# Expert products in halves of 512 columns, the scatter matrix by one comparison, and 22 large buffers

## The chip, the cores and the metric

The kernel runs on one core of one Trainium2 chip. The metric is the device time of one execution in microseconds (us). Before the change three runs took 841.2, 843.68 and 844.19 us; the median is 843.68. The engines are named as in the profile: PE is TensorE (matmuls; its weight loads are listed as PEld), DVE is VectorE, ACT is ScalarE, POOL is GpSimd, SP is SyncE, which issues the DMA transfers here.

## The reference

One decoder block on x of 512 tokens by 1024 channels, all float32: a first RMS norm, one input projection, a pooling mixer and a differential attention, two gates, an output projection with residual. Then the part that the change touches, a hierarchical mixture of 32 experts, of which each token uses two of one group:

```python
hn = rmsnorm(x, norm2_g)                      # 512 x 1024
pg = softmax(hn @ w_rg + b_rg)                # 4 groups, the best one is taken
pe = softmax((hn @ w_re + b_re)[its group])   # 8 experts, the best two
wts = p_top * pv / sum(pv)
hdn = silu(xb @ w_gate[e]) * (xb @ w_up[e])   # xb: the rows of hn that go to e; 1024 -> 512
y = (hdn @ w_down[e]) * wb                    # 512 -> 1024
out = x + (y added at its token's row)
```

## The kernel before

**Stages.** The first stage computes norm, projection, attention, pooling and output projection with float32r products in three passes (high and low parts of both operands). Its weights are loaded by `stage_to` (L141) and split into high and low parts by ACT and DVE in `split_to` (L154 and L155). Then come the router and the experts.

**The expert loop.** It begins at L1026 and takes the experts in 16 pairs, 0 to 15. Each expert has 64 slots (CAP); what goes beyond them is done in `run_overflow`, a loop that stands behind pair 6 (P_OVER) and takes as many turns as there are full blocks left, none with these inputs. The two experts of a pair share every PSUM bank: one has the upper 64 partitions, the other the lower 64.

Four experts form a group. `prep_P` builds the one-hot matrix P (token by slot) of a group with DVE, and `gather` (L851) multiplies hn with it on PE, which gives xT, the group's tokens by channel; this is done in the odd pairs for the next group. For a pair, in PE's order:

- gate and up (`ffn_in`, L881): 16 float32 matmuls each of 64 weight columns by 512 moving columns. The profile counts two records for each float32 matmul, so 32.
- `scatter_mats`: four matmuls with the identity (tile tp, L861) transpose P into PT, slot by token, copied by DVE (L863); four small matmuls (tile ws, L867) collect the slots' routing weights, which DVE adds into wv (L873).
- the gather of the next group, in odd pairs.
- `ffn_hT`: h = silu(gate) * up comes from ACT (L885) and DVE (L887); PE transposes it (ht, L894), DVE copies it to hT (L896).
- the last quarter of the pair before, scattered.
- `quarter_down` (L907), four quarters of 256 output columns: y on PE, its high part by ACT (L910), the low part by DVE (L911).
- `quarter_scatter` (L921), one quarter behind: PT times the high and the low part for four token blocks, in two banks; DVE adds each bank to the accumulator acc (L923).

**What sets the order.** The program is written out in its final order, and each engine works through its own list in order; semaphores come from the tile framework. Buffers are pools of equal tiles: 23 large ones of 8 KB a partition (tag S), 6 small ones of 2 KB (tag T) and 8 PSUM banks. A tile takes a buffer that is free in program order, and its first writer waits until the last reader of the old tile is done. In the expert loop acc, hn and xT hold five large buffers and the weight tiles the rest, 18. `prefetch(4)` stands behind gate, behind up and at the pair's end and issues four loads each time on SP's queue (L618); the first eighteen are issued in `out_proj` by the counts in PF. A pair uses twelve tiles: four each for gate, up and down. The last pair's down weights come as eight half tiles, one for each expert and quarter.

Of the kernel before, what the change touches and what calls it, by code (L numbers as in the profile page):

```python
# [27 lines left out]
CAP = 64  # L28
# [7 lines left out]
NBIG = 23  # L36
NSM = 6
# [4 lines left out]
PF = (6, 4, 3, 5)  # L42
# [5 lines left out]
def hybrid_block_kernel(  # L48
# [65 lines left out]
    # ---------------------------------------------------------------- loads  # L114
# [58 lines left out]
    # ---------------------------------------------------------------- constants  # L173
# [66 lines left out]
    # ---------------------------------------------------------------- first norm and transposes  # L240
# [24 lines left out]
    # ---------------------------------------------------------------- products in three float32r passes  # L265
# [20 lines left out]
    # ---------------------------------------------------------------- q, k, v  # L286
# [25 lines left out]
    # ---------------------------------------------------------------- attention  # L312
# [104 lines left out]
    # ---------------------------------------------------------------- pooling  # L417
# [28 lines left out]
    # ---------------------------------------------------------------- phase 1 program  # L446
# [146 lines left out]
    # ---------------------------------------------------------------- expert weights  # L593
# [27 lines left out]
    # ---------------------------------------------------------------- output projection, second norm, router  # L621
# [13 lines left out]
    Wst = const.tile([128, NT, NE, 2], F16, name="Wst")  # L635
# [199 lines left out]
    # ---------------------------------------------------------------- experts  # L835
# [5 lines left out]
    def gather(P, n, t0, t1, st, ks=(0, 1)):  # L841
        per = 512 // n
        if t0 == 0 and 0 in ks:
            st["b"] = [bank("xg", (128, per, n)) for _ in range(ND // per)]
            st["x"] = S([128, ND, n], name="xT") if ND * n > 512 else \
                T("xT")[:, :ND * n].rearrange("p (j s) -> p j s", j=ND)
        for k in ks:
            for i, b in enumerate(st["b"]):
                for t in range(t0, t1):
                    for j in range(per):  # L850
                        mm(b[:, j, :], hn[k][:, t, i * per + j, :], P(t),  # L851
                           start=t + k + j == 0, stop=t == NT - 1 and k == 1 and j == per - 1)
                if t1 == NT and k == 1:
                    jj = slice(i * per, (i + 1) * per)
                    tt(st["x"][:, jj, :], b, g2p[:, jj, None].to_broadcast([128, per, n]), op=OP.mult)
        return st["x"]

    def scatter_mats(Pp, np_, w):
        b = bank("tp", (128, 4, 128))
        for t in range(NT):  # L860
# [3 lines left out]
        bw = bank("ws")  # L864
        ne = w.shape[2]
        for t in range(NT):
            mm(bw[:np_, :2 * ne], Pp(t), w[:, t].rearrange("p e k -> p (e k)"), start=t == 0, stop=t == NT - 1)  # L867
        ws = small([128, 4], "ws")
        nc.vector.tensor_copy(ws[:np_, :2 * ne], bw[:np_, :2 * ne])
        wv = small([128, 1], "wv")  # L870
        for par in range(ne):
            s = slice(par * CAP, (par + 1) * CAP)
            ts(wv[s], ws[s, 2 * par:2 * par + 1], ws[s, 2 * par + 1:2 * par + 2], 1.0 / W_SCALE, op0=OP.add, op1=OP.mult)  # L873
        return PT, wv
# [16 lines left out]
    def ffn_hT(h, np_):  # L891
# [4 lines left out]
        nc.vector.tensor_copy(hTt[:, :, :np_], b[:, :, :np_])  # L896
# [29 lines left out]

    def take(w, e, part):
# [16 lines left out]
    # ---- blocks beyond the first CAP slots of an expert  # L944
# [33 lines left out]
    def run_overflow():  # L978
# [13 lines left out]
        with tc.For_i(0, n_over, 1) as i:  # L992
            e = nc.values_load(ov_i[0:1, ds(i, 1)], min_val=0, max_val=NE - 1)
            ts(rcol, R1[:, :, ds(e, 1)].rearrange("p t o -> p (t o)"), offs[:, ds(i, 1)], None, op0=OP.subtract)
            nc.vector.tensor_copy(wcol, Wst[:, :, ds(e, 1), :].rearrange("p t o k -> p t (o k)"))
# [29 lines left out]

    for p in range(NE // 2):  # L1026
# [3 lines left out]
        c0 = (p % 2) * 2 * CAP  # L1030
        xs = [st["x"][:, :, c0 + par * CAP:c0 + (par + 1) * CAP] for par in range(2)]
        bg_ = bank("gate")
# [3 lines left out]
        following = {}  # L1036
        if p % 2 == 1 and g + 1 < NE // 4:
            prep_P(g + 1, 0, NT, following)
# [12 lines left out]
        last_pair = p == NE // 2 - 1  # L1051
        halves = None if last_pair else [take("d", e, half) for half in range(2)]
        yq = {}
        for q in range(4):
            w = take("q", e, q) if last_pair else halves
            yq[q] = quarter_down(hTt, wv, w, q, 128)
            if q > 0:
                quarter_scatter(PT, q - 1, yq[q - 1], 128, last_pair)
        prev = (PT, 3, yq[3], 128, last_pair)
# [5 lines left out]
    quarter_scatter(*prev)  # L1065
# [25 lines left out]
```

## Time and profile before

| | |
|---|---|
| median of three runs | 843.68 us |
| span of the profiled execution | 844.5 us |
| that execution's own time | not given beside its span |
| PE busy | 813.4 us |
| DVE busy | 385.3 us |
| ACT busy | 202.5 us |
| moved by DMA | 234.15 MB |
| mean granted clock | 0.989 |

The span is the time from the first to the last instruction on the core. Busy time of an engine counts overlapping instructions once. Matmuls are pipelined: one lasts longer than the distance between two starts, so a mean duration is not what a matmul costs in a stream. The chain that ended last is followed back from the last instruction: at each step to what released it, or to the instruction before it on its engine. "Idle before" names the time in which the engine had nothing to do before an instruction, and what ended it. The granted clock is a share of TensorE's full 2.4 GHz.

### The profile page before, as it was taken

Reading aid. Unit: us, or ns where it says so; the run is one execution under the profiler, and the core shown is the slowest. Engines: PE = TensorE matmul, PEld = TensorE weight load, DVE = VectorE, ACT = ScalarE, POOL = GpSimd, SP = SyncE. Lnnn points to the kernel's source line nnn. Section 1 sums busy time; section 2 is a strip of 40 time slices with the busy share of each in tenths; the row PEclk is TensorE's granted clock in tenths of the full one; section 3 lists DMA queues with packets and bytes.
Section 4 is the critical chain, followed back from the end, with each engine's and each line's share of the span. In section 5 each row is a group of like instructions: output and inputs, shape, how many; then the busy total and the mean of one; then the engine's idle time right before and its main releaser. Section 6 shows DMA issues by size and latency. Waiting matters only on the chain. (4 is left out here: it accounts for less than half of the span.)

```text
span 844.5 us, 11816 instructions
## 1 busy us (share of the span) xinstructions
PE 813.4 (96%) x4822; PEld 531.8 (63%) x4822; DVE 385.3 (46%) x851; ACT 202.5 (24%) x405; POOL 36.4 (4%) x48
## 2 busy tenths in 40 slices
PE   7999999999999998999999999979999999999997
PEld 6887767778888877456456456446456456457444
DVE  5644495553555535743554244333253244335225
ACT  5544455445433424200010010000000010010010
POOL 1220050000000000000000000000000000000000
PEclk9999999999999999999999999989999999999999
DMA  9611103213266818589899999979999999999922
GB/s 317 208 51 50 50 11 111 79 50 100 88 226 252 331 50 331 210 328 426 352 426 426 379 425 424 385 285 427 386 427 425 382 426 426 381 427 425 410 74 100
DMA packets 54008, 234.15 MB, mean 277 GB/s; under 512 B 9920, under 2 KB 16576, under 8 KB 29888
## 3 DMA queue, kind: packets, MB, share of 16 engines
q1 hardware_dynamic: 53952, 233.37, 68.9%
q8 instruction: 39, 0.64, 0.3%
q14 instruction: 17, 0.14, 0.0%
HBM read 231.26 MB, written 2.10 MB: 276 GB/s over the span
## 5 line engine op out<-in xcount | busy, mean ns | idle before, releaser
L907 PE MATMUL y<-e,hT 128*64 128x256 f32 x1024 | 122.8, 388 | 3.2 <-DVE hT L896 3.2
L881 PE MATMUL gate<-e,xT 128*64 128x512 f32 x512 | 115.2, 603 | 4.9 <-DVE P L838 4.9
L881 PE MATMUL up<-e,xT 128*64 128x512 f32 x512 | 112.6, 592 | 0.0
L910 ACT ACTIVATE yq<-y,wv 128x256 fp32r<-128x256 f32 x64 | 30.4, 475 | 318.0 <-PE y L907 318.0
L887 DVE TENSOR_TENSOR h<-up,sg 128x512 f32<-128x512 f32 x16 | 17.0, 1062 | 183.2 <-PE up L881 113.5
L907 PEld LDWEIGHTS y<-e,hT 128*64 128x64 f32 x1024 | 70.1, 138 | 41.6 <-DVE hT L896 6.4
L881 PEld LDWEIGHTS up<-e,xT 128*64 128x64 f32 x512 | 36.7, 137 | 73.2 <-issue 73.2
L923 DVE TENSOR_TENSOR acc<-sc,acc 128x512 f32<-128x512 f32 x128 | 81.8, 681 | 0.2
L881 PEld LDWEIGHTS gate<-e,xT 128*64 128x64 f32 x512 | 35.8, 139 | 72.5 <-issue 69.7
L921 PE MATMUL sc<-yq,PT 128*128 128x256 f32 x512 | 77.4, 294 | 0.0
L921 PEld LDWEIGHTS sc<-yq,PT 128*128 128x128 f32 x512 | 64.8, 189 | 18.5 <-issue 18.5
L911 DVE SCALAR_TENSOR_TENSOR yq<-y,wv,yq 128x256 fp32r<-128x256 f32 x64 | 30.9, 484 | 86.9 <-ACT yq L910 86.9
L155 DVE SCALAR_TENSOR_TENSOR wl<-w,g1c,wh 128x512 fp32r<-128x512 f32 x64 | 48.9, 792 | 39.0 <-ACT wh L154 38.9
L282 PE MATMUL g<-hTh,wh 128*128 128x512 f32 x160 | 64.8, 405 | 0.1
L284 PE MATMUL g<-hTh,wl 128*128 128x512 f32 x160 | 62.4, 390 | 0.0
L283 PE MATMUL g<-hTl,wh 128*128 128x512 f32 x160 | 62.4, 390 | 0.0
L851 PE MATMUL xg<-P,hn 128*128 128x256 f16 x512 | 58.0, 272 | 0.5 <-DVE hn L672 0.4
L851 PEld LDWEIGHTS <-hn 128*128 128x128 f16 x512 | 49.2, 98 | 8.7 <-issue 2.1
L154 ACT ACTIVATE wh<-w,g1c 128x512 fp32r<-128x512 f32 x64 | 44.5, 719 | 1.0 <-DMA w<-in_w_in_dram 1.0
L885 ACT ACTIVATE sg<-gate 128x512 f32<-128x512 f32 x16 | 9.6, 597 | 122.3 <-PE gate L881 122.3
L282 PEld LDWEIGHTS g<-hTh,wh 128*128 128x128 f32 x160 | 30.0, 188 | 13.1 <-issue 5.4
L284 PEld LDWEIGHTS g<-hTh,wl 128*128 128x128 f32 x160 | 30.0, 188 | 6.5
(212 smaller groups left out, 983.6 us busy)
## 6 DMA issues: line engine op xcount, KB each, us to landing
e<-in_w_expert_gate_dram SPq DMA_DIRECT2D x64, 1024.0 KB, 10.1
e<-in_w_expert_up_dram SPq DMA_DIRECT2D x64, 1024.0 KB, 11.5
e<-in_w_expert_down_dram SPq DMA_DIRECT2D x60, 1024.0 KB, 13.7
w<-in_w_in_dram SPq DMA_DIRECT2D x16, 1024.0 KB, 5.4
w<-in_w_out_dram SPq DMA_DIRECT2D x4, 1024.0 KB, 5.8
e<-in_w_expert_down_dram SPq DMA_DIRECT2D x8, 512.0 KB, 9.0
x<-in_x_dram SPq DMA_DIRECT2D x4, 512.0 KB, 6.3
w<-in_w_pool_up_dram SPq DMA_DIRECT2D x2, 1024.0 KB, 4.8
```

The lines of the kernel that those rows point to most:

```text
L154: nc.scalar.mul(hi, src, g)
L155: stt(lo, src, g, f(hi), op0=OP.mult, op1=OP.subtract)
L282: mm(b, whi[:, k, s], ahi[:, k, :], start=first and k == 0, stop=False)
L283: mm(b, whi[:, k, s], alo[:, k, :], start=False, stop=False)
L284: mm(b, wlo[:, k, s], ahi[:, k, :], start=False, stop=last and k == 3)
L851: mm(b[:, j, :], hn[k][:, t, i * per + j, :], P(t), start=t + k + j == 0, stop=t == NT - 1 and k == 1 and j == per - 1)
L881: mm(b[s, :], xs[par][:, j, :], w[par][:, k, :], start=j == 0, stop=j == 7)
L907: mm(y[s, :], hTt[:, j, s], r, start=j == 0, stop=j == 3)
L910: nc.scalar.mul(yhl[:np_, 0], y[:np_], wv[:np_])
L911: stt(yhl[:np_, 1], y[:np_], wv[:np_], f(yhl[:np_, 0]), op0=OP.mult, op1=OP.subtract)
L921: mm(b[:, i, :], PT[:np_, t * 128:(t + 1) * 128], yhl[:np_, k, :], start=k == 0, stop=k == 1)
L923: tt(a, b, a, op=OP.add)
```

## The change

Pairs 0 to 14 compute the down product in two halves of 512 columns (`half_down`) instead of four quarters of 256. Each half is scattered by token blocks (`scatter_mms`), one bank for each block of 128 tokens, the high and the low part on the same weights. The first half is scattered behind both halves of y; the second is kept for the next pair, where three of its blocks stand behind up and the fourth behind ht. The four additions stand behind hT in the program. Pair 15 keeps its quarters.

PT is no longer transposed on PE. The weights tile Wst gets a third column, the token's number from 1 (`tok_id`, built by POOL); the ws matmuls (now `slot_info`, six columns) bring it to the slots along with the weights, and `scatter_mat` compares a row of all token numbers (`tok_row`) with it, in one DVE operation of 128 by 512. slot_info is called for both pairs of a group at once: in pair 0 for the first group, then in odd pairs behind the gather. hT is copied by ACT instead of DVE. P of the next group is built before gate instead of behind it. There are 22 large buffers instead of 23 and 8 small ones instead of 6; the last count of PF is 4 instead of 5, so 17 weight tiles are under way.

```diff
-NBIG = 23
-NSM = 6
+NBIG = 22
+NSM = 8
-PF = (6, 4, 3, 5)
+PF = (6, 4, 3, 4)
...
-    Wst = const.tile([128, NT, NE, 2], F16, name="Wst")
+    Wst = const.tile([128, NT, NE, 3], F16, name="Wst")
+    tok_id = const.tile([128, NT], F32, name="tok_id")
+    nc.gpsimd.iota(tok_id, pattern=[[128, NT]], base=1, channel_multiplier=1, allow_small_or_imprecise_dtypes=True)
+    nc.gpsimd.tensor_copy(Wst[:, :, :, 2], tok_id[:, :, None].to_broadcast([128, NT, NE]))
+    tok_row = const.tile([128, SEQ], F32, name="tok_row")
+    nc.gpsimd.iota(tok_row, pattern=[[1, SEQ]], base=1, channel_multiplier=0, allow_small_or_imprecise_dtypes=True)
...
-    def scatter_mats(Pp, np_, w):
-        b = bank("tp", (128, 4, 128))
+    def slot_info(P, e):
+        bw = bank("ws")
         for t in range(NT):
-            mm(b[:np_, t, :], Pp(t), ident_h, start=True, stop=True)
+            mm(bw[:, :6], P(t), Wst[:, t, e:e + 2, :].rearrange("p e k -> p (e k)"), start=t == 0, stop=t == NT - 1)
+        ws = small([128, 6], "ws", bufs=4)
+        nc.vector.tensor_copy(ws, bw[:, :6])
...
+    def scatter_mat(ws):
         PT = T("PT")[:, :SEQ].bitcast(F32R)
-        nc.vector.tensor_copy(PT[:np_], b[:np_].rearrange("p a b -> p (a b)"))
+        ts(PT, tok_row, ws[:, 2:3], None, op0=OP.is_equal)
+        return PT
...
-        nc.vector.tensor_copy(hTt[:, :, :np_], b[:, :, :np_])
+        copy(hTt[:, :, :np_], b[:, :, :np_])
...
+    def half_down(hTt, wv, w, hf):
+        y = bank("y")
+        for j in range(4):
+            for par in range(2):
+                r = slice(par * CAP, (par + 1) * CAP)
+                mm(y[r, :], hTt[:, j, r], w[j // 2][par][:, j % 2, hf * 512:(hf + 1) * 512], start=j == 0, stop=j == 3)
+        hi, lo = (T(n)[:, :512].bitcast(F32R) for n in ("yh", "yl"))
+        nc.scalar.mul(hi, y, wv)
+        stt(lo, y, wv, f(hi), op0=OP.mult, op1=OP.subtract)
+        return hi, lo
+
+    def scatter_mms(PT, hf, y2, t):
+        b = bank("sc")
+        for k in range(2):
+            mm(b, PT[:, t * 128:(t + 1) * 128], y2[k], start=k == 0, stop=k == 1)
+
+        def add():
+            a = acc_t(t)[:, hf * 512:(hf + 1) * 512]
+            tt(a, b, a, op=OP.add)
+        return add
...
         h = ffn_h(bg_, bu, 128)
-        PT, wv = scatter_mats(lambda t: P_of(st)(t)[:, c0:c0 + 2 * CAP], 128, Wst[:, :, e:e + 2, :])
-        if following:
-            gather(P_of(following), 4 * CAP, 0, NT, following)
-            groups[g + 1] = following
-        hTt = ffn_hT(h, 128)
+        adds = [scatter_mms(*prev, t) for t in range(3)] if prev else []
+        if p == 0:
+            infos(0)
+        hTt = ffn_hT(h, 128, nc.scalar.copy)
         if prev:
-            quarter_scatter(*prev)
...
+            adds.append(scatter_mms(*prev, 3))
+        for add in adds:
+            add()
+        PT = scatter_mat(info[p][0])
+        wv = info[p][1]
+        if p % 2 == 1 and more:
+            gather(P_of(groups[g + 1]), 4 * CAP, 0, NT, groups[g + 1])
+            infos(g + 1)
...
+        halves = [take("d", e, half) for half in range(2)]
+        y0 = half_down(hTt, wv, halves, 0)
+        y1 = half_down(hTt, wv, halves, 1)
+        for t in range(NT):
+            scatter_mms(PT, 0, y0, t)()
+        prev = (PT, 1, y1)
```

What moves is shown for pair 8. First PE between up and the first y matmul, before (tp is P transposed, yq and PT are those of pair 7 in the sc rows, e the weights):

```order
L861 MATMUL tp_5065<-ident_h,P_4776 128x128
L867 MATMUL ws_5072<-Wst,P_4776 128x4
L894 MATMUL ht_5082<-ident,h_5063 128x128 x4
L921 MATMUL sc_5089<-yq_4988,PT_4815 128x256 x4
L921 MATMUL sc_5095<-yq_4988,PT_4815 128x256 x4
L907 MATMUL y_5101<-e_4772,hT_5087 64x256
```

And after (yh, yl and PT in the sc rows are those of pair 7):

```order
L949 MATMUL sc_4740<-yh_4658,PT_4541 128x512
L949 MATMUL sc_4740<-yl_4659,PT_4541 128x512
L949 MATMUL sc_4743<-yh_4658,PT_4541 128x512
L949 MATMUL sc_4743<-yl_4659,PT_4541 128x512
L949 MATMUL sc_4746<-yh_4658,PT_4541 128x512
L949 MATMUL sc_4746<-yl_4659,PT_4541 128x512
L902 MATMUL ht_4749<-ident,h_4738 128x128 x4
L949 MATMUL sc_4756<-yh_4658,PT_4541 128x512
L949 MATMUL sc_4756<-yl_4659,PT_4541 128x512
L940 MATMUL y_4765<-e_4487,hT_4754 64x512
```

The transposes of P and the ws matmuls are gone from here; six matmuls of the scatter left over stand ahead of ht and two behind it, where a quarter's eight stood behind it. Next DVE in the same pair, from h on, before:

```order
L887 TENSOR_TENSOR h_5063<-up_5036,sg_5061 128x512
L863 CAST PT_5070<-tp_5065 128x512
L869 COPY ws_5077<-ws_5072 128x4
L873 TENSOR_SCALAR wv_5079<-ws_5077 64x1 x2
L896 COPY hT_5087<-ht_5082 128x512
L923 TENSOR_TENSOR acc_2197<-sc_5089,acc_2197 128x2x256
L923 TENSOR_TENSOR acc_2198<-sc_5095,acc_2198 128x2x256
L911 SCALAR_TENSOR_TENSOR yq_5110<-y_5101,wv_5079,yq_5110 128x256
```

And after:

```order
L895 TENSOR_TENSOR h_4738<-up_4711,sg_4736 128x512
L953 TENSOR_TENSOR acc_2197<-sc_4740,acc_2197 128x512
L953 TENSOR_TENSOR acc_2197<-sc_4743,acc_2197 128x512
L953 TENSOR_TENSOR acc_2198<-sc_4746,acc_2198 128x512
L953 TENSOR_TENSOR acc_2198<-sc_4756,acc_2198 128x512
L881 TENSOR_SCALAR PT_4763<-tok_row,ws_4621 128x512
L943 SCALAR_TENSOR_TENSOR yl_4775<-y_4765,wv_4623,yh_4774 128x512
L943 SCALAR_TENSOR_TENSOR yl_4788<-y_4778,wv_4623,yh_4787 128x512
L953 TENSOR_TENSOR acc_2197<-sc_4791,acc_2197 128x512
```

Between h and the first low part of y DVE had the copy of PT, the ws and wv operations, the copy of hT and two additions; now it has four additions and the comparison that makes PT. The copy of hT stands on ACT, between sg of this pair and yh.

## Rows read from the trace of the kernel before

**Rows 1.** The page, part 1: busy us of each engine, share of the span, instructions.
```profile
PE 813.4 (96%) x4822; PEld 531.8 (63%) x4822; DVE 385.3 (46%) x851; ACT 202.5 (24%) x405; POOL 36.4 (4%) x48
```

**Rows 2.** The page, part 4: the chain that ended last, by line.
```profile
PE y L907 8%; PE gate L881 8%; PE up L881 7%; PE sc L921 4%; PE xg L851 3%; DVE hT L896 0%; DVE PT L863 0%; DVE wv L873 0%; PE ht L894 0%; DVE P L838 0%; PE tp L861 0%; DVE acc L923 0%; DVEq L1087 0%; DVEq L992 0%; ACT yq L910 0%
```

**Rows 3.** The chain in order of time, pairs 8 and 9: start us, us, what.
```profile
598.84 7.02 PE gate L881 x32
...
615.83 3.67 PE y L907 x32
619.50 1.15 PE sc L921 x8
620.65 1.88 PE y L907 x16
...
626.70 7.02 PE gate L881 x32
...
640.59 0.33 PE tp L861 x4
...
648.44 0.95 PE sc L921 x8
...
660.26 7.02 PE gate L881 x32
```

**Rows 4.** Timeline, pair 8: start, us, instruction, [idle before <- releaser].
```profile
612.86 1.05 DVE L887 TENSOR_TENSOR h<-up,sg 128x512 f32<-128x512 f32 x1 [12.91 <-PE up L881]
...
613.97 0.66 PE L894 MATMUL ht<-ident,h 128*128 128x128 f32 x4 [0.84 <-DVE h L887]
...
615.08 0.69 DVE L896 COPY hT<-ht 128x512 f32<-128x512 f32 x1
```

**Rows 5.** The page, part 6: DMA issues, count, KB each, median us to landing.
```profile
e<-in_w_expert_gate_dram SPq DMA_DIRECT2D x64, 1024.0 KB, 10.1
...
w<-in_w_in_dram SPq DMA_DIRECT2D x16, 1024.0 KB, 5.4
```

**Rows 6.** Stretches: us, PE busy (count), granted clock, DMA share, GB/s.
```profile
340.00:344.00 4.00, 2.98 (x25) 1.00 0.00 0
...
358.00:364.00 6.00, 3.69 (x28) 0.86 1.01 427
...
620.00:640.00 20.00, 20.00 (x118) 1.00 1.01 426
```

**Rows 7.** Timeline of PE in the first stage, first and last of twelve.
```profile
205.39 0.39 PE L282 MATMUL g<-yTh,wh 128*128 128x512 f32 x1
...
207.89 0.39 PE L284 MATMUL g<-yTh,wl 128*128 128x512 f32 x1
```

**Rows 8.** Groups by form: count, busy us, mean ns, idle before.
```profile
L680 ACT COPY xgT<-th 128x512 f32<-128x512 f32 x8 | 4.6, 573 | 1.7 <-PE th L679 1.7
...
L399 DVE SCALAR_TENSOR_TENSOR oTl<-to,cols,oTh 128x512 fp32r<-128x512 f32 x4 | 3.0, 745 | 0.2 <-ACT oTh L398 0.2
...
L398 ACT ACTIVATE oTh<-to,cols 128x512 fp32r<-128x512 f32 x4 | 2.7, 686 | 5.3 <-PE to L396 5.3
...
L224 DVE TENSOR_SCALAR bias<-dist 128x512 f32<-128x512 f32 x4 | 1.4, 416 | 0.0
```

**Rows 9.** Timeline around the overflow loop behind pair 6.
```profile
558.26 1.28 DVE L923 TENSOR_TENSOR acc<-sc,acc 128x512 f32<-128x512 f32 x2
560.25 2.17 SPq L618 DMA_DIRECT2D e<-in_w_expert_gate_dram  x4
...
563.36 1.12 PE L881 MATMUL gate<-e,xT 128*64 128x512 f32 x2 [4.92 <-DVE P L838]
```

**Rows 10.** Timeline of PE in pair 0.
```profile
359.78 0.66 PE L894 MATMUL ht<-ident,h 128*128 128x128 f32 x4 [0.79 <-DVE h L887]
...
361.64 5.36 PE L907 MATMUL y<-e,hT 128*64 128x256 f32 x32 [1.20 <-DVE hT L896]
```

**Rows 11.** The page, part 5: the weights' split, idle before it and releaser.
```profile
L154 ACT ACTIVATE wh<-w,g1c 128x512 fp32r<-128x512 f32 x64 | 44.5, 719 | 1.0 <-DMA w<-in_w_in_dram 1.0
```

More of the change, by code (lines that the diff above doesn't have):

```diff
@@ L839, in make_P, with gather @@
            op=OP.is_equal)
-    def gather(P, n, t0, t1, st, ks=(0, 1)):
+    def gather(P, n, t0, t1, st, ks=(0, 1), part=None):
         per = 512 // n
+        if t0 == 0 and 0 in ks and part in (None, 0):
+            st["x"] = S([128, ND, n], name="xT")
+        which = range(ND // per) if part is None else range(2 * part, 2 * part + 2)
         if t0 == 0 and 0 in ks:
-            st["b"] = [bank("xg", (128, per, n)) for _ in range(ND // per)]
-            st["x"] = S([128, ND, n], name="xT") if ND * n > 512 else \
-                T("xT")[:, :ND * n].rearrange("p (j s) -> p j s", j=ND)
+            st.setdefault("b", {}).update({i: bank("xg", (128, per, n)) for i in which})
         for k in ks:
-            for i, b in enumerate(st["b"]):
+            for i in which:
+                b = st["b"][i]
                 for t in range(t0, t1):
@@ L856, in gather @@
         return st["x"]
-    def scatter_mats(Pp, np_, w):
-        b = bank("tp", (128, 4, 128))
+    def slot_info(P, e):
+        bw = bank("ws")
         for t in range(NT):
-            mm(b[:np_, t, :], Pp(t), ident_h, start=True, stop=True)
-        PT = T("PT")[:, :SEQ].bitcast(F32R)
-        nc.vector.tensor_copy(PT[:np_], b[:np_].rearrange("p a b -> p (a b)"))
[L864 to L874, printed above, removed]
+            mm(bw[:, :6], P(t), Wst[:, t, e:e + 2, :].rearrange("p e k -> p (e k)"), start=t == 0, stop=t == NT - 1)
+        ws = small([128, 6], "ws", bufs=4)
+        nc.vector.tensor_copy(ws, bw[:, :6])
+        wv = small([128, 1], "wv", bufs=4)
+        for par in range(2):
+            r = slice(par * CAP, (par + 1) * CAP)
+            ts(wv[r], ws[r, 3 * par:3 * par + 1], ws[r, 3 * par + 1:3 * par + 2], 1.0 / W_SCALE, op0=OP.add,
+               op1=OP.mult)
+        return ws, wv
+    def scatter_mat(ws):
+        PT = T("PT")[:, :SEQ].bitcast(F32R)
+        ts(PT, tok_row, ws[:, 2:3], None, op0=OP.is_equal)
+        return PT
     def ffn_in(b, xs, w, half):
@@ L889, in ffn_h, with ffn_hT @@
         return h
-    def ffn_hT(h, np_):
+    def ffn_hT(h, np_, copy):
         b = bank("ht", (128, 4, 128))
@@ L1024, in run_overflow, with infos @@
                 quarter_scatter(PT, q, yq, CAP, False, banks[6])
+    info = {}
+    def infos(g):
+        for par in range(2):
+            c = par * 2 * CAP
+            st = groups[g]
+            info[2 * g + par] = slot_info(lambda t: P_of(st)(t)[:, c:c + 2 * CAP], 4 * g + 2 * par)
     for p in range(NE // 2):
@@ L1035, in hybrid_block_kernel @@
         prefetch(4)
-        following = {}
-        if p % 2 == 1 and g + 1 < NE // 4:
-            prep_P(g + 1, 0, NT, following)
         bu = bank("up")
@@ L1043, in hybrid_block_kernel @@
         h = ffn_h(bg_, bu, 128)
-        PT, wv = scatter_mats(lambda t: P_of(st)(t)[:, c0:c0 + 2 * CAP], 128, Wst[:, :, e:e + 2, :])
-        if following:
-            gather(P_of(following), 4 * CAP, 0, NT, following)
-            groups[g + 1] = following
-        hTt = ffn_hT(h, 128)
-        if prev:
-            quarter_scatter(*prev)
[L1051 to L1059, printed above, removed]
+        adds = [scatter_mms(*prev, t) for t in range(3)] if prev else []
+        if p == 0:
+            infos(0)
+        hTt = ffn_hT(h, 128, nc.scalar.copy)
+        if prev:
+            adds.append(scatter_mms(*prev, 3))
[3 more added lines that the diff above has]
+        wv = info[p][1]
+        if p % 2 == 1 and more:
+            gather(P_of(groups[g + 1]), 4 * CAP, 0, NT, groups[g + 1])
+            infos(g + 1)
+        if last_pair:
+            yq = {}
+            for q in range(4):
+                yq[q] = quarter_down(hTt, wv, take("q", e, q), q, 128)
+                if q > 0:
+                    quarter_scatter(PT, q - 1, yq[q - 1], 128, True)
+            quarter_scatter(PT, 3, yq[3], 128, True)
+            break
+        halves = [take("d", e, half) for half in range(2)]
[4 more added lines that the diff above has]
+        prev = (PT, 1, y1)
         if p == P_OVER:
```

9 lines of the change are left out of this document (7 added, 2 removed).

## The prediction

> **What bounds the kernel now.** Four views, from wide to narrow. The page's first part: TensorE (PE) is busy 96% of the span, VectorE (DVE) 46% [rows 1]. That figure alone proves nothing, so next the chain that ended last: it runs through PE's y, gate, up, sc and xg, with a few tenths of a per cent on DVE and no weight transfer in it [rows 2]. In order of time the chain shows the period of the expert pairs [rows 3]: an even pair lasts from 598.84 to 626.70, 27.86 us; an odd one, which also gathers the next four experts, from 626.70 to 660.26, 33.56 us. Inside the even pair PE works without a pause except in one place: up ends at 612.8, where h starts on DVE, and y starts at 615.83. The timeline of that gap [rows 4] shows why: h must be computed (1.05 us) before ht can be transposed, and hT is copied at 615.08 only, because PT and the ws and wv operations stand ahead of it on DVE. PE fills some 0.95 us of these 3.06 us with a scatter quarter and about as much with tp, ws and ht.
>
> Last, the transfers. A weight tile is 1,024 KB [rows 5]; where the DMA share is 1.01, 426 GB/s are moved, over 20 us at a stretch [rows 6], so a tile takes 2.46 us and a pair's twelve tiles 29.5 us. Two pairs take PE 61.4 us and the transfers 59.0: PE bounds the loop, but by 4% only. Every microsecond taken from PE has to be checked against the transfers.
>
> **The change, part by part.** Pairs are numbered 0 to 15.
>
> *Down product (y).* Four quarters now: 3.67 + 1.88 + 1.88 = 7.43 us [rows 3]. Half products have the shape of the gate product (64 weight columns, 512 moving columns, float32), 32 records in 7.02 us. So 7.02 us, 0.41 less a pair.
>
> *Scatter (sc).* A quarter is 8 records of 256 columns, 1.15 us [rows 3]. A half is 8 of 512 columns with the same weights. The trace has no such sc, but this form in the first stage: eleven starts between 205.39 and 207.89, 0.227 us each [rows 7]. A half is then 1.82 us. Behind y stood three quarters (3.45), now one half: 1.63 less. Bounds: 0.22 us by the gate records (7.02/32), and 0.287 if two 256-column records cost what they cost now, which gives 2.30 a half and leaves 1.15 of this saving. I take 0.227, the same form. The Trainium skill (TensorE: Matmul & The Clock Gate, Back-to-back issue gap) has an isolated gap of N/2.4 + 2.5 ns, 216 ns for 512 columns; the row is at 227. By the page the saving would be some 3 us larger, 812.
>
> *The gap of the even pair.* tp goes, ws moves to the odd pairs, hT goes to ScalarE (ACT). After up PE now has three token blocks of the half left over, 6 x 0.227 = 1.36 us; h, done 1.1 us after up's end, is ready by then. ht takes 0.66 until its last result, ACT starts about 0.06 later, its copy takes 0.57 as the same copy in the router does [rows 8], and the wait 0.04: y starts 2.69 after up instead of 3.06, 0.37 less. The fourth block lies beside the copy. ACT has nothing else queued between sg and hT. The four additions to acc, 0.64 each [rows 9], stand behind h on DVE and end about 4 us after up; PT follows by a comparison, 0.42 us as the one-operand operation of this size takes [rows 8]; it is first read when both halves of y are done, over 9 us after up, so both are hidden. If that cover went, PT's 0.42 would count. Bounds for the gap: 2.2 us (the PE work alone) to 3.56 (as late as now, plus the half us more of scatter in front).
>
> Even pair: 0.41 + 1.63 + 0.37 = 2.41 less, 25.45 us.
>
> *Odd pair.* y and the tail of sc again give 2.04; tp's 0.33 goes; the sc block in front grows from 0.95 to 1.82; ws grows by four matmuls, an estimate of 0.08 from tp's four in 0.33, most of it their 128 columns. The hT copy was and is hidden behind xg. 2.04 + 0.33 - 0.87 - 0.08 = 1.42 less, 32.14 us. The ws copies and wv operations come behind xT on DVE, beside y's first half. On SP's queue the loads stand where they stood, behind gate, up and the pair's end.
>
> *Pair 0.* Nothing is left over in front, and ws for two pairs fits before h. hT, on ACT right behind ht (359.78), lets y start at 361.1 instead of 361.64: 0.53. With y and sc 2.57. At present PE idles 0.79 us before ht and 1.20 before this y, the granted clock of the stretch falls to 0.86 (part of it at 1.2 GHz), and the 32 records last 5.36 us instead of 3.67 [rows 6, 10]; some 1.6 are to be won if it stays at 2.4 GHz. Of the 1.20 about 0.7 stays; in the even pairs, with 0.84 before ht [rows 4] and little before y, the clock held. In between, so half: 3.4 less, 2.6 to 4.2.
>
> *The drain behind pair 6.* The overflow loop, which runs no turn, waits for every engine and transfer. Now DVE's last two additions end at 559.54 [rows 9], some 1.1 us behind PE's last matmul. After the change the second half's yh (0.69) and yl (0.75) [rows 8] and four additions (2.6) follow y, 4.2 us with the handovers against 1.82 of sc: 2.4 behind PE instead of 1.1, 1.3 us worse. The transfers end at about the same time (below).
>
> *Pair 15* keeps its quarters; only its gap shrinks, 0.4 less.
>
> *Two more small tiles* free nothing that anyone waits for in these rows: 0. *tok_row and tok_id* are built on GpSimd, busy 4% of the span [rows 1], long before use: 0. *One large buffer less* in the first stage: a load takes its buffer when the last reader has left it. The loads are far ahead now: the split of the weights waited 1.0 us in all for a load [rows 11]. I take 0; at worst one load is late by its whole 5.4 us [rows 5].
>
> *Sum:* 7 x 2.41 (pairs 2, 4 to 14) + 7 x 1.42 (1, 3 to 13) + 3.4 + 0.4 - 1.3 = 29.3 us. From the profiled span of 844.5 that leaves 815.2. The page gives that execution no time beside its span; the median of the three runs is 0.8 us lower. I predict 815.
>
> **Do the transfers keep up?** PE's mean pair is now 28.8 us, less than their 29.5. They are ahead at the start: between 340 and 344 nothing moves [rows 6], so all that was issued has landed, and the first gate has not begun. With 17 tiles instead of 18 they can be 5 tiles, 12.3 us, ahead beyond the pair in work. Up to the drain four even pairs cost them 4.1 each and three odd ones give back 2.6: 8.6. After it 95 tiles have landed and 84 are used up. The 93rd after that is the last up tile of pair 15: 93 x 2.46 us, and 3 more until it has landed (a lone load lands 5.4 after its issue [rows 5]), is 232 after the drain. PE resumes about 3 us after the loads do [rows 9] and wants it 4 x 32.1 + 4 x 25.5 us, gate and half of up (10.5) and some 2 of slow clock later, at 246. So 14 us to spare; below 400 GB/s it is gone.
>
> **The rivals.**
> *The transfers become the bound.* For it: 4% is all that lies between, and there is one tile less. Against: 426 GB/s over 20 us with PE busy throughout [rows 6]. At 380 GB/s a tile takes 2.76 us and that tile would come 14 us late: 829. The Trainium skill (DMA: Bandwidth & Descriptors, Where 436 GB/s comes from) says that HBM binds such loads at about 358 GB/s a core. By that rule the 93rd tile comes 29 us late and the time is 844, no change; the row at 426 contradicts it here.
>
> *The gap does not shrink.* The scatter in front pushes ht and hT back, and y starts 0.87 later than now. Then an even pair gains 1.17 only: 815.2 + 7 x 1.24 = 824. For it: the blocks now stand ahead of ht on an in-order engine. Against: h needs 1.1 of their 1.36 us anyway.
>
> *Slower.* One mechanism: in each pair 1 to 14 PE waits for hT as long as in pair 0 now, 0.79 + 1.20 us, and the clock falls to 1.2 GHz as there, 1.6 more. With the 0.4 us that PE idles there anyway that is 14 x (2.0 - 0.4 + 1.6) = 45 us more: 860. It decides when the idle time around ht reaches those 2.0 us. For it: the chain PE, DVE, PE, ACT, PE is still one of four handovers. Against: PE has 1.82 us of scatter in it, and the gaps of the even pairs left the clock alone.
>
> *It does not do what it says:* same period because records of 512 columns cost twice those of 256. Only the gap and tp would be won, about 10 us: 835. The gate and first-stage rows speak against it.
>
> **How the numbers follow.** Forecast 815: 0.73, with its own range 811 to 820 (scatter spacing, pair 0's clock, the drain). Gap not shrunk, 824: 0.10. Transfers, 820 to 844: 0.10. No gain from width, 835: 0.03. Slower, 860: 0.04. To leave two in ten out, the range is 808 to 828. Less than 0.5% (4 us) is about what a measurement of this kernel cannot tell from none: faster than 839.5 has 0.92, within 0.5% 0.04 (the far end of the transfer case), slower 0.04.
>
> **What would show it.** In the changed profile an even pair of 25.4 us and an odd one of 32.1; y x32 at 7.0; eight sc of 512 columns in 1.8; y starting 2.7 after up, released by ACT's hT; no wait of PE for an e tile; idle time at the drain some 1.3 us more behind the last sc. An even pair of 26.7 means the gap stayed. Waits of gate or up for an e transfer, the DMA share at 1.00 to the end and a pair of 29.5 mean the transfers took over. A clock under 1.00 inside a pair is the slower case.

## The result, and the profile of the changed kernel

The changed kernel takes 817.43 us, the median of four runs (814.21 to 821.59); beside it the kernel before takes 843.93. The ratio is 0.968, 95% interval 0.965 to 0.971. Forecast: 815, range 808 to 828. The execution that was profiled is the slowest of the four, 821.59 us with a span of 819.8, so 1.8 us lie around the span. TensorE's mean granted clock is 0.989 in the slowest run and 0.998 in the fastest.

The page's first part, busy us of each engine [rows 1]:

```profile
PE 797.1 (97%) x4038; PEld 479.1 (58%) x4038; DVE 365.6 (45%) x805; ACT 204.0 (25%) x391; POOL 37.3 (5%) x51
```

784 matmuls are gone, and PE's busy time falls by 16 us. The chain by line is still one of PE, with less than half a per cent each on ACT and DVE, and no weight transfer in it.

The chain in order of time, an even pair (8) and an odd one (9) [rows 3]; start us, us, what:

```profile
585.30 7.02 PE gate L889 x32
592.32 6.87 PE up L889 x32
599.18 1.59 PE sc L949 x6
600.77 0.45 PE ht L902 x4
...
601.30 0.59 ACT hT L904
...
601.94 7.09 PE y L940 x32
609.02 2.07 PE sc L949 x8
611.09 7.02 PE gate L889 x32
618.11 6.87 PE up L889 x32
624.98 1.59 PE sc L949 x6
626.57 0.43 PE ht L902 x4
627.00 0.47 PE sc L949 x2
627.48 7.00 PE xg L858 x64
634.48 0.18 PE ws L869 x8
634.66 7.02 PE y L940 x32
641.68 2.04 PE sc L949 x8
```

The even pair lasts 25.79 us (27.86 before, 25.45 forecast), the odd one 32.63 (33.56, 32.14 forecast). y starts 2.76 us behind the end of up, released by ACT's hT. The gap from closer, in the timeline of all engines [rows 4] (start, us, instruction, idle before it and who ended it):

```profile
599.11 0.19 PEld L949 LDWEIGHTS sc<-yh,PT 128*128 128x128 f32 x1 [0.81 <-issue]
599.11 0.50 PE L949 MATMUL sc<-yh,PT 128*128 128x512 f32 x1
...
599.33 1.07 DVE L895 TENSOR_TENSOR h<-up,sg 128x512 f32<-128x512 f32 x1 [12.14 <-PE up L889]
599.45 0.40 PE L949 MATMUL sc<-yl,PT 128*128 128x512 f32 x1
599.45 0.19 PEld L949 LDWEIGHTS sc<-yh,PT 128*128 128x128 f32 x1
...
599.68 0.39 PE L949 MATMUL sc<-yh,PT 128*128 128x512 f32 x1
...
600.32 2.48 DVE L953 TENSOR_TENSOR acc<-sc,acc 128x512 f32<-128x512 f32 x4
...
602.71 0.48 DVE L881 TENSOR_SCALAR PT<-tok_row,ws 128x512 fp32r<-128x512 f32 x1
```

Two things are to be seen. Inside a block of scatter the matmuls start every 0.23 us, as forecast (599.45 to 599.68). But the first one of the block needs 0.34 (599.11 to 599.45): its weights (PEld) are loaded only when it starts, while those of the later ones are loaded under the matmul ahead of them. And h, the four additions and PT lie on VectorE as forecast, far ahead of the first reader of PT at 609.02.

Stretches of PE [rows 6] (us, PE busy, granted clock, DMA share, GB/s):

```profile
358.00:364.00 6.00, 4.04 (x28) 1.00 1.02 429
...
620.00:640.00 20.00, 20.00 (x134) 1.00 1.01 420
```

The clock did not fall in pair 0 this time, and the transfers run at 420 GB/s, a tile in 2.50 us. PE's timeline at the stop behind pair 6 [rows 9], with VectorE's last additions:

```profile
546.13 2.48 DVE L953 TENSOR_TENSOR acc<-sc,acc 128x512 f32<-128x512 f32 x4
546.35 0.39 PE L949 MATMUL sc<-yl,PT 128*128 128x512 f32 x1
549.70 1.12 PE L889 MATMUL gate<-e,xT 128*64 128x512 f32 x2 [2.96 <-DVEq L1021]
...
550.06 1.43 DVE L843 TENSOR_TENSOR P<-slot,R 128x256 f16<-128x256 f32 x4 [1.45 <-issue]
```

VectorE's first work behind the stop is P of the next group. In the kernel before it stood here, with the gate product at 563.36 [rows 9]:

```profile
560.98 1.43 DVE L838 TENSOR_TENSOR P<-slot,R 128x256 f16<-128x256 f32 x4 [1.45 <-issue]
```

With the starts of the 16 gate products, read from PE's timeline in both traces, the whole difference of the spans can be laid out:

| Stretch (gate to gate) | before, us | after, us | difference | forecast |
|---|---|---|---|---|
| start to the first gate | 344.17 | 345.37 | +1.20 | 0 |
| pair 0 | 29.96 | 26.08 | -3.88 | -3.4 |
| six even pairs (2, 4, 8 to 14) | 167.12 | 154.59 | -12.53 | -14.5 |
| six odd pairs (1, 3, 5, 9 to 13) | 201.40 | 195.79 | -5.61 | -8.5 |
| pair 6 with the stop | 32.81 | 28.81 | -4.00 | -1.1 |
| pair 7 | 35.41 | 35.53 | +0.12 | -1.4 |
| pair 15 and the end | 33.63 | 33.63 | 0.00 | -0.4 |
| sum | 844.5 | 819.8 | -24.7 | -29.3 |

Pair 7 gained nothing: in both executions the gate behind the stop starts at 1.2 GHz, with a granted clock of 0.50 from 564 to 567 in the kernel before and, for longer, from 549 to 555 in the changed one. The other odd pairs take 33.56 and 32.63.

### The profile page after: what moved, and what is told of

Read it like the earlier page. It is cut to its first block, busy times and chain, and to the rows that moved or that the text cites. A ratio compares the mean times of both kernels' runs of the same rounds, so it can differ in the third digit from the quotient of the medians.

```text
span 819.8 us, 10177 instructions
## 1 busy us (share of the span) xinstructions
PE 797.1 (97%) x4038; PEld 479.1 (58%) x4038; DVE 365.6 (45%) x805; ACT 204.0 (25%) x391; POOL 37.3 (5%) x51
## 5 line engine op out<-in xcount | busy, mean ns | idle before, releaser
L940 PE MATMUL y<-e,hT 128*64 128x512 f32 x480 | 106.3, 595 | 2.5 <-ACT hT L904 2.5
L953 DVE TENSOR_TENSOR acc<-sc,acc 128x512 f32<-128x512 f32 x120 | 74.2, 681 | 0.0
L940 PEld LDWEIGHTS y<-e,hT 128*64 128x64 f32 x480 | 33.1, 137 | 65.8 <-issue 59.1
L943 DVE SCALAR_TENSOR_TENSOR yl<-y,wv,yh 128x512 fp32r<-128x512 f32 x30 | 22.5, 751 | 85.1 <-ACT yh L942 82.4
L942 ACT ACTIVATE yh<-y,wv 128x512 fp32r<-128x512 f32 x30 | 20.6, 688 | 146.2 <-PE y L940 146.2
L949 PE MATMUL sc<-yh,PT 128*128 128x512 f32 x120 | 51.5, 430 | 0.0
L949 PE MATMUL sc<-yl,PT 128*128 128x512 f32 x120 | 47.3, 394 | 0.0
L904 ACT COPY hT<-ht 128x512 f32<-128x512 f32 x16 | 9.4, 586 | 126.3 <-PE ht L902 126.3
L949 PEld LDWEIGHTS sc<-yh,PT 128*128 128x128 f32 x120 | 22.5, 188 | 27.6 <-issue 24.3
## 6 DMA issues: line engine op xcount, KB each, us to landing
e<-in_w_expert_up_dram SPq DMA_DIRECT2D x64, 1024.0 KB, 14.5
```

Of the source, the lines that this page charges most:

```text
L940: mm(y[r, :], hTt[:, j, r], w[j // 2][par][:, j % 2, hf * 512:(hf + 1) * 512], start=j == 0, stop=j == 3)
L942: nc.scalar.mul(hi, y, wv)
L943: stt(lo, y, wv, f(hi), op0=OP.mult, op1=OP.subtract)
L949: mm(b, PT[:, t * 128:(t + 1) * 128], y2[k], start=k == 0, stop=k == 1)
L953: tt(a, b, a, op=OP.add)
```

## The experiments

All ratios are to the kernel before, run on the same chip beside them. "Even" and "odd" are the lengths of such pairs from gate to gate.

**The changed kernel again (after_again).**

> The changed kernel unaltered, as the yardstick of this chip. Both theories: 817 us as before, ratio to the kernel before 0.968; in its profile an even pair of 25.8 us and an odd one of 32.6, whatever the number of stretches at 1.2 GHz outside the pairs.

Measured: 817.93 us (814.65 to 820.16), ratio 0.966 (0.963 to 0.969); even 25.79, odd 32.63. This profiled execution has a span of 817.0. Its pair 7 takes 32.60 in place of 35.53, since the gate behind the stop ran at 2.4 GHz at once; its pair 0 takes 27.70 in place of 26.08, with y at 1.2 GHz in part. PE's timeline and the stretch (columns as above):

```profile
360.93 8.74 PE L940 MATMUL y<-e,hT 128*64 128x512 f32 x32 [0.68 <-ACT hT L904]
```
```profile
358.00:366.00 8.00, 6.04 (x27) 0.79 1.01 424
```

What follows: the pairs repeat to 0.03 us. Pair 0 and pair 7 differ from run to run by 1.6 and 2.9 us for the same instructions and, to 0.1 us, the same idle time.

**The width undone (q_quarters).**

```
-        y0 = half_down(hTt, wv, halves, 0)
-        y1 = half_down(hTt, wv, halves, 1)
-        for t in range(NT):
-            scatter_mms(PT, 0, y0, t)()
-        prev = (PT, 1, y1)
+        for q in range(4):
+            yq[q] = quarter_down(hTt, wv, halves, q, 128)
+            if q > 0:
+                quarter_scatter(PT, q - 1, yq[q - 1], 128, False)
+        prev = (PT, 3, yq[3], 128, False)   # half of it ahead of ht, half behind
```

> The changed kernel with the down product and the scatter of pairs 0 to 14 in quarters of 256 columns again; the comparison for PT, hT on ScalarE and the buffers stay. Theory (the width is worth its matmul time): three quarters of sc behind y, 3.45 us, in place of 2.05, y 7.43 in place of 7.05, and a gap from up to y of some 2.45 in place of 2.76 because only half a quarter lies ahead of ht. Even pair 27.3 us, odd pair 34.0, in all some 20 us more: 837. Rival (the width is worth nothing, the gap and tp made the gain): even pair as now, 25.8 us, and 817. Second rival (the weight transfers set the pace of the changed kernel, and PE time given back only fills waits): less than 6 us more, 823 at most.

Measured: 844.76 us, ratio 0.9986 (0.9970 to 1.0003): no change from the kernel before. Even 27.34, as expected, odd 34.23, 0.2 more; the stop behind pair 6 costs PE 5.03 us in place of 2.9, which was not expected. The time is 8 us above the 837. The profile shows where, beside that of after_again if not said otherwise: 1.6 in the odd pairs (against the expected 34.0), 2.1 at the stop, 1.7 in pair 0 (27.79 against 26.1 in the changed kernel, both at a clock of 1.00), 1.4 in a slow gate behind the stop (pair 7 35.60) and 1.4 ahead of the first gate (345.32 against 343.94). The chain of an even pair behind up, and the gate behind the stop from the timeline:

```profile
612.70 1.07 DVE h L895
...
613.81 0.67 PE ht L902 x4
...
614.50 0.59 ACT hT L904
...
615.14 3.67 PE y L915 x32
```
```profile
562.99 1.12 PE L889 MATMUL gate<-e,xT 128*64 128x512 f32 x2 [5.03 <-issue]
```

h itself stands in the chain: the half quarter ahead of ht no longer covers it. PE waits for h in all 16 pairs, 9.3 us in sum. What follows: the comparison, ScalarE's copy and 22 buffers without the width are worth nothing. They take 0.5 us from an even pair (27.86 to 27.34) and put 0.68 on an odd one (33.55 to 34.23), where ht now stands ahead of xg and waits for h in the open. The three blocks of the half that stand there in the changed kernel are what hides this wait.

**The comparison undone (pt_transposed).**

```
-        ts(PT, tok_row, ws[:, 2:3], None, op0=OP.is_equal)
+        for t in range(NT):
+            mm(b[:, t, :], Pp(t), ident_h, start=True, stop=True)
+        nc.vector.tensor_copy(PT, b.rearrange("p a b -> p (a b)"))
```

> The changed kernel with PT made as before, by four transposes of P on PE and a copy by VectorE, at the place of the comparison (behind the scatter's last block, ahead of y or xg). Theory (the comparison is worth PE's time for tp and nothing else): in odd pairs and pair 0's like the four tp cost 0.33 us and a change of product, 0.4 us; in even pairs 0.26 of it lies in PE's wait for hT, 0.15 us remain. 7 x 0.4 + 8 x 0.15 = 4 us more: 821.5, ratio to the kernel before 0.971. Rival (PT's copy comes late for the scatter behind the additions): sc behind y waits for VectorE, seen in the profile. Second rival (the tp lie beside waits everywhere): 817.5.

Measured: 817.86 us, ratio 0.9681 (0.9660 to 0.9702). Even 25.71, odd 32.83: nearest to the second rival, but the odd pair is 0.2 longer. The chain of an even pair:

```profile
599.90 0.47 PE sc L952 x2
600.37 0.24 PE tp L882 x4
600.61 7.05 PE y L943 x32
```

The four tp take 0.24 us, and in even pairs they lie in the 0.26 us for which PE would wait for hT. In odd pairs they cost 0.2. In sum the comparison is worth some 1 us by the pairs, too little to be seen in the times.

**hT later, on VectorE (ht_dve_late), and hT at once, on VectorE (ht_dve_first).**

```
-        hTt = ffn_hT(h, 128, nc.scalar.copy)
+        bh = ffn_hT_mm(h)                      # the four transposes only
         ...
         for add in adds:
             add()
+        nc.vector.tensor_copy(hTt, bh)         # ht_dve_late
```
```
-        hTt = ffn_hT(h, 128, nc.scalar.copy)
+        hTt = ffn_hT(h, 128, nc.vector.tensor_copy)   # ht_dve_first, ahead of the additions
```

> The changed kernel with hT copied by VectorE, behind the four additions to acc, in place of ScalarE. Theory: in an even pair the additions end 3.6 us after up does, the copy takes 0.57, so y starts 4.25 us after up in place of 2.76: 1.5 us more in each of 7 even pairs and about 0.5 in pair 0; in odd pairs the copy lies beside xg and costs nothing. 11 us more: 828. PE then idles some 1.75 us before y and the clock stays at 2.4 GHz. Rival (the slower case of the prediction: an idle stretch of about 2 us makes the granted clock fall, as in pair 0 of the kernel before): besides these 1.5 the y product behind each gap loses 1.6 us more, an even pair of 28.9 us, 840.

> The changed kernel with hT copied by VectorE right behind h, ahead of the four additions. Theory (the place in the queue makes the gap, not the engine): y starts 2.76 us after up as now, even pair 25.8 us, odd pair 32.6, PT 0.6 later and still hidden: 817. Rival (ScalarE's free queue is what shrank the gap, since VectorE would have to finish the additions that wait for sc): y 1 us later or more, even pair 26.8 or above, 825.

Measured: ht_dve_late 833.32 us, ratio 0.986 (0.984 to 0.989); even 27.28, odd 32.61. The even pair is 1.5 longer, as the theory had it, and y still takes 7.09:

```profile
606.28 0.68 DVE acc L959
606.96 0.61 DVE hT L1098
...
607.61 7.09 PE y L946 x32
```

The clock stayed at 1.00 in these pairs although PE was idle for 1.8 us in each: the slower case of the prediction does not come at this size. The time is 5 us above the expectation. Beside after_again the profile shows 1.5 more in pair 15 (35.1 in place of 33.6, overlooked), 1.7 in a slow gate behind the stop (pair 7 34.30 against 32.61) and 1.7 ahead of the first gate (345.66 against 343.94), while pair 0 is 1.1 shorter. ht_dve_first, a single execution of 821.79 us: even 25.82, odd 32.60. The engine makes no difference, the place in the queue does. Only pair 0 suffers, where the copy then stands behind ws and wv: it lasts 29.54 us, y waits 1.27 in place of 0.68, and the granted clock of the stretch is the lowest of all runs:

```profile
358.00:366.00 8.00, 6.05 (x20) 0.61 1.01 424
```

The wait alone does not do that: in ht_dve_late this y waits 1.28, the clock stays at 1.00, and pair 0 lasts 26.65.

**One block of scatter more (sc_split).**

```
             ffn_in(bg_, xs, take("g", e, half), half)
+            if half == 0 and later:
+                for t in range(2, NT):
+                    scatter_mms(*later, t)()
```

> The changed kernel with the eight sc behind y cut in two blocks: four stay behind y, four come between the two halves of the next gate product (pairs 1 to 6 and 8 to 14). Theory (each block of scatter among 64-column products costs 0.2 us at its own front and 0.15 at the front of the product behind it, whatever its length): one block more a pair, 0.35 us, even pair 26.1, odd pair 33.0, 13 x 0.35 = 4.5 us more: 822. Rival (the 0.2 us are a wait for yh, yl or PT right behind y, which a block in the middle of gate does not have): even pair 25.8, time as of the changed kernel, 817.5.

Measured: 821.74 us, ratio 0.973 (0.971 to 0.975). Even 26.15, odd 33.01, 0.37 and 0.38 more than in the changed kernel. The chain of an even pair behind y:

```profile
610.31 1.14 PE sc L949 x4
611.45 3.58 PE gate L889 x16
615.03 1.14 PE sc L949 x4
616.18 3.58 PE gate L889 x16
```

Four sc cost 1.14, twice that is 2.28 and not 2.07; two halves of gate cost 7.16 and not 7.02. So in the chain, which counts from end to end, a block costs 0.2 us of its own and about 0.15 in what follows, also in the middle of gate, where it waits for nothing.

**Blocks joined (sc_late), and fewer tiles asked for at the stop (late_hold4, late_hold4_fill).**

```
-        adds = [scatter_mms(*prev, t) for t in range(3)] if prev else []
+        left = [scatter_mms(*prev[i], t) for i, t in BLOCKS[:3]] if prev else []   # BLOCKS: both halves, eight blocks
         hTt = ffn_hT(h, 128, nc.scalar.copy)
-            adds.append(scatter_mms(*prev, 3))
+            left += [scatter_mms(*prev[i], t) for i, t in BLOCKS[3:]]
 ...
-        for t in range(NT):
-            scatter_mms(PT, 0, y0, t)()
-        prev = (PT, 1, y1)
+        prev = ((PT, 0, y0), (PT, 1, y1))
 
-HOLD = 2
+HOLD = 4                                       # late_hold4, late_hold4_fill
```

> The changed kernel with all eight token blocks of the scatter (both halves) moved behind the next pair's up product: six matmuls ahead of ht, ten behind it, none behind y. Theory (each change of PE to and from a block of scatter costs about 0.1 us, because the first weights are loaded only when the product before has ended; the width of the block costs 0.233 a matmul): two such changes less a pair, 0.2 us, and in even pairs the 0.26 us that PE still waits for hT are filled: even pair 25.3, odd pair 32.4, together with a drain 2 us shorter some 6 us less: 811. Rival (the extra 0.22 us of a scatter block belong to the matmuls, not to the change): only the 0.26 of the even pairs and the drain, 4 us less, odd pair 32.6. Second rival: VectorE's eight additions in a row (0.62 each) hold up the sc banks and the y product, PE waits about 1 us a pair: 830.

> The kernel sc_late (all eight token blocks of the scatter behind the next up) with four tiles instead of two held back at pair 6 until the overflow loop is through. In sc_late PE waits 6.8 us there, until the last transfer that has been asked for is in. Theory (what sc_late gained in the pairets, 0.68 us an even and 0.38 an odd pair, was paid back at this wait): two tiles of 2.49 us less to wait for, the wait 6.8 to 2.5 us, 4 us less than sc_late: 812; behind it the tiles held back still come in time. Rival: the wait shrinks, but the two tiles come late behind it, PE waits for them in pairs 7 to 9, and the time stays 816.

> The kernel late_hold4 with the ten filling matmuls of fill0 in pair 0. Theory (what late_hold4 won is 0.66 us an even and 0.35 an odd pair and a stop behind pair 6 of 2.6 us, and it comes again on another chip): even pair 25.1, odd pair 32.3, pair 6 27.8, ratio to the kernel before 0.963, 812 us. Rival (the difference of 0.963 to the 0.966 to 0.968 of the changed kernel was chance of the clock): ratio 0.967, 815.5.

Measured: sc_late 816.4 us, ratio 0.965 (0.962 to 0.967). Even 25.11, odd 32.25, better than expected (25.3, 32.4). The chain of pair 9:

```profile
604.91 6.87 PE gate L889 x32
...
618.64 1.59 PE sc L949 x6
620.23 0.44 PE ht L902 x4
620.67 2.30 PE sc L949 x10
```

The gate product behind y takes 6.87 us where behind sc it took 7.02, and ten sc take 2.30, just 0.23 each. But only some 1.5 of the 7 us that the pairs won arrived. In the profile pair 6 with the stop is 3.3 us longer than in after_again (32.07 against 28.75), and pair 7 is 2.7 longer (35.28 against 32.61, with a slow gate behind the stop). PE's waits at the stop, of sc_late and of late_hold4:

```profile
PE gate L889 <- SPq L1021: 6.8, 1, 6.8
```
```profile
PE gate L889 <- SPq L1021: 2.6, 1, 2.6
```

In sc_late PE comes to the stop early and waits there for the last transfers, which move 348 GB/s up to 542 and next to nothing behind that, with the gate at 544.36:

```profile
540.00:542.00 2.00, 0.00 (x0) 0.53 0.85 348
542.00:544.00 2.00, 0.00 (x0) 0.50 0.19 78
```

With two more tiles held back, pair 6 shrinks from 32.07 to 27.84 us, and no later pair waits for a tile: 813.27 us, ratio 0.963 (0.961 to 0.965). With the filling matmuls of fill0 (below) in pair 0 it is 812.39 us, ratio 0.961 (0.958 to 0.963), with the same pairs (25.1, 32.3, pair 6 27.9). These two are faster than the changed kernel (0.966 and 0.968 in its two measurements) by about half a per cent; the intervals of single measurements touch, the lengths of the pairs do not.

**Fewer tiles ahead (ahead_0).**

```
-PF = (6, 4, 3, 4)
+PF = (6, 4, 3, 0)
```

> The changed kernel with 13 weight tiles asked for ahead of the first gate instead of 17, buffers as they are. Theory (the transfers, 12 x 2.49 = 29.9 us a pair against 29.2 of PE, are kept in front only by the tiles ahead): without these four the pairs become as long as their transfers, PE waits for an e tile in several pairs, 5 to 10 us more: 822 to 827. Rival (of the 14 us to spare that the prediction counted four are left, and PE never waits): 817.5, no wait for an e tile. Second rival (transfers set the end of the loop already): 4 x 2.49 = 10 us more or above, 828.

Measured: 820.56 us, ratio 0.9725 (0.970 to 0.975). Every pair up to 14 is as long as in the changed kernel (25.78, 32.61); only pair 15 lasts 35.75 us in place of 33.64, and there alone PE waits for a tile:

```profile
PE up L889 <- DMA e<-in_w_expert_up_dram: 1.0, 1, 1.0
```

Four tiles (10 us) less cost 2.1 us at the last up product. So the changed kernel had about 8 us to spare there, an estimate from this one run: neither theory's number, and nearest to the first rival.

**No stop (no_loop).** The overflow loop, which runs no turn here, is left out.

```
-        if p == P_OVER:
-            run_overflow()
```

> The changed kernel without the overflow loop behind pair 6 (with this input it runs no turn); the two tiles held back there are still held back. Theory (the stop costs PE 3.0 us of idle time behind pair 6, and in part of the runs the gate behind it starts at 1.2 GHz, up to 2.9 us more): the stretch from gate to gate of pair 6 goes from 28.8 to 25.8 us, that of pair 7 is 32.6 in every run, 3.0 to 5.9 us less: 813. Rival (the transfers have nothing left to spare, and what PE gains it waits for at the end): pair 15 longer by as much, 817.

Measured: 815.43 us, ratio 0.965 (0.961 to 0.969). Pair 6 takes 25.77 in place of 28.75 to 28.81, pair 7 32.62, pair 15 33.31. By the profile the stop costs 3.0 us, and up to 2.9 more when the clock is down behind it. The time alone, 2.5 us less than after_again, would not have settled it.

**Pauses of pair 0 filled (fill0).** Ten matmuls of the identity, results unused, go ahead of ws (4), of ht (3) and of y (3).

> The changed kernel with ten matmuls of the identity put into PE's three pauses of pair 0 (ahead of ws, of ht and of y), their results unused. Theory (the idle time in pair 0 is what makes the granted clock fall there in a part of the runs: the stretch from gate to gate of pair 0 was 26.1 us in two profiled runs of kernels with this pair and 27.7 in two others): with the pauses filled pair 0 lasts 26.1 us in every run, and the mean clock of the runs rises from 0.994 to 0.996, some 0.7 us less: 816.5 to 817. Rival (the fall has another cause, such as the slow stretches of the output projection before it): pair 0 still falls in half of the runs, mean clock 0.994, 817.5.

Measured: 815.76 us, ratio 0.967 (0.964 to 0.970); pair 0 26.17 us at a clock of 1.00. But this execution shows no fall ahead of the first gate either, where those with a fall in pair 0 have one, so it tells little. Mean clocks of the six runs: 0.993, 0.994, 0.994, 0.998, 0.999, 0.999; of after_again 0.990, 0.990, 0.992, 0.994, 0.996, 0.998. These were taken on two chips, and the kernel before differs between the same two chips by as much (0.993 and 0.990 in the mean). So it does not settle the theory.

## Why the prediction was right, and where it was not

*Right in time and cause.* The gain is the width: with quarters it is gone to within 0.3%, with everything else of the change in place (q_quarters). That the time came within 2.4 us is in part luck, since misses of both signs met: in the table above the twelve pairs away from the stop gained 18.1 us in place of 23.0, and pair 6 with the stop 4.0 in place of 1.1.

*y:* 7.02 us forecast, 7.02 to 7.09 measured. *Records of 512 columns:* 0.227 us forecast, 0.23 measured, so the case that wide records cost double is out.

*The scatter, mis-sized.* The prediction counted a half as 8 x 0.227 = 1.82 and the six matmuls in front as 1.36. They cost 2.04 to 2.07 and 1.59: 0.2 us for each block come on top. The first matmul, whose weights aren't loaded under the one ahead, takes 0.11 of it (0.34 in place of 0.23). The rest lies at the block's end: behind y the last sc starts at 610.70 and gate at 611.02, 0.32 later; the reason for that is not shown. The row for this was there: a quarter's 1.15 us [rows 3] already held such a front, but the spacing was taken from the middle of a row of equal matmuls [rows 7]. sc_split adds one block and pays 0.37 us; sc_late joins blocks and gets it back. In an even pair the block behind y is 0.25 over the forecast and the gap 0.07, in an odd pair the two blocks are 0.22 and 0.24 over; that makes 5.5 us over 14 pairs, most of what the forecast gained too much there (0.34 an even and 0.49 an odd pair, 5.8 us). (The Trainium skill, TensorE: Matmul & The Clock Gate, Architectural detail, says that PE's queue can pull weight loads ahead of matmuls in flight. Inside a block the trace agrees; at the change from up's 128*64 tiles to the scatter's 128*128 the load waited, with 0.81 us without any load ahead of it.)

*The gap:* 2.69 forecast, 2.76 measured, ended by ACT's hT as forecast. Two misses nearly cancel in it: the six sc take 1.59 in place of 1.36, and from there to the start of ACT's copy it takes 0.53 (600.77 to 601.30) in place of 0.72. The reason given, that hT is no longer queued behind other work, holds (ht_dve_late: +1.5), and that ScalarE does it is no part of it (ht_dve_first). That tp's 0.33 us would be saved in odd pairs did not hold: at their place in the changed kernel they cost 0.2 there, and in even pairs they lie in a wait (pt_transposed).

*Pair 0:* 3.4 forecast, 3.88 measured. The prediction counted half of a fall of the clock; the profiled execution had none, which is luck. Of nine profiled executions with the same three pauses in pair 0, to 0.25 us (after, after_again, pt_transposed, sc_split, ahead_0, no_loop, sc_late, late_hold4, q_quarters), three show the fall (after_again, pt_transposed, no_loop) and six don't. In the changed kernel the pair takes 26.1 without it and 27.7 with it, so a gain of 3.9 or of 2.3. What decides is open. In the three with a fall, and in ht_dve_first, the clock had also fallen some 24 us earlier, ahead of the first gate; in the others it had not. The kernel before, with 1.20 us ahead of y, fell here without such an earlier fall; it was profiled once, so whether it always does is not known.

*The drain, wrong in sign.* The prediction put it 1.3 us worse, since VectorE ends later behind PE. That half is true: the last addition ends 1.9 us behind PE's last matmul in place of 1.1. But the rest of the stop, from that addition to the first gate, took 3.8 us before (559.54 to 563.36) and takes 1.1 now (548.61 to 549.70), so PE's idle time falls from 4.92 to 2.96. The step took this rest for a constant of the loop. It is 1.0 to 1.1 in all kernels with halves that don't wait for a transfer there, and 3.9 in q_quarters (559.06 to 562.99). VectorE is out of the loop equally fast, 1.45 us after its last addition, before (560.98) and after (550.06); it is PE that starts 2.4 us behind VectorE before and 0.4 ahead of it after. Weight transfers are not the reason: in the kernel before next to nothing moves from 555 to 560 (25 GB/s at most in any microsecond). Nor does the fetching of instructions fill the time: 16 KB come in on the instruction queue (q8 in the trace's DMA packets) at the end of the stop, and in the kernel before the last of them is in at 560.79, 2.6 us ahead of the gate. Why PE comes out later with quarters stays open; the additions, the loop and what follows are alike.

*Transfers.* 426 GB/s forecast, 420 measured, and 8 us to spare where 14 were counted. (The Trainium skill's page DMA: Bandwidth & Descriptors, Where 436 GB/s comes from, has HBM bind at about 358; the trace, with this one core at work, disagrees: 420 GB/s over 20 us.) The prediction looked for the next bound only at the end of the loop. It stands earlier, at the stop, where all transfers asked for must have landed: in the changed kernel they end there together with VectorE, and sc_late, 0.66 us faster in an even and 0.32 in an odd pair, ran into them.

*What lay outside:* the output projection was at 1.2 GHz for longer in the profiled execution of the changed kernel (granted clock 0.66 over 320 to 330, 0.83 before), and the first gate came 1.2 us later; first gates came between 340.7 and 345.7 us in all runs. The 22 buffers show no cost; no run puts the 23rd back. Pair 15 gained nothing in place of 0.4: its gap did shrink, from 3.06 to 2.75, but from VectorE's last addition to the end of the span it took 3.8 us in place of 3.5.

## What to carry to other kernels

Price a block of matmuls as a fixed cost plus a spacing: here 0.2 us of its own, 0.15 in its successor, and 0.23 for each matmul of 512 columns; so join blocks, and read the fixed cost from a block's whole length in the trace. When work is pulled forward on an in-order engine, check what used to cover its wait, and put other ready work there. Before a stop that waits for all transfers, ask for fewer of them, or a faster loop only waits there longer.

## What the runs showed that had not been expected

- The granted clock in pair 0 and behind the stop differs between runs of the same instructions with the same idle time (pair 0 26.1 or 27.7 us, pair 7 32.6 or 35.5), while 1.8 us of idle time in each of seven even pairs never lowered it.
- Four fp16 transposes of 128 columns cost 0.24 us behind a block of scatter with full-width weights, against 0.33 behind up's narrow tiles in the kernel before.
- From the last addition through a loop that runs no turn to the first matmul behind it took PE 1.1 us in one form of the code and 3.8 in another, while VectorE's way was the same 1.45 in both.
